# Moving all of GpSimd's work but a triangular inversion to ScalarE and VectorE in a hybrid decoder step

## The chip, the cores and the metric

One NeuronCore of one Trainium2 chip runs the whole program. The metric is device time in microseconds (us) from the first to the last instruction of one execution, with the small fixed part around it that the timer also sees. Lower is better. The times before come from three executions; the trace comes from one further execution with the hardware profiler on.

## The reference

One layer of a decoder runs over 1024 prompt tokens and 8 single-token samples, all in float32. RMSNorm of x, one input projection (1024 to 7688 columns), and then three branches whose outputs are gated, merged and projected back. The branch that this change touches is the gated delta branch:

```python
qkv, new_buf = causal_conv(conv_buf, concat([q, k, v]), conv_w)   # 4 taps, then SiLU
q = l2norm(q) * DK ** -0.5 ; k = l2norm(k)
L    = where(strict, (k * beta) @ k.T * decay, 0)                 # per chunk
Tinv = triangular_solve(eye + L, eye)                             # inverse of a lower triangle
u = Tinv @ (v * beta) ; w = Tinv @ (k * beta * exp(gc))
for each chunk:                                                   # state S: 128x128 per head
    v_new = u - w @ S
    o = q_dec @ S + attn @ v_new
    S = S * g_last + k_dec.T @ v_new
```

There are 4 heads of 128 by 128. For the 8 samples the same rule runs for one token on a given state (`state_delta`), and the new state is an output.

## The kernel before, in words

**Projections.** All heavy matmuls are float32 split in two rounded halves (hi and lo), so each output tile of 128 columns takes three passes over 8 contraction blocks (`mm3`, L299 to L304), for three groups of 344 tokens: 24 matmuls a group, 72 a job. A job's weights come by an ACT-queue DMA (`w_load`, L265), are cast to hi on ScalarE (L277) and subtracted to lo on VectorE (L280). Each group's PSUM bank (`pj`, two of them) is emptied by ScalarE or VectorE before a third group can use it.

**Order of the work.** The schedule is written out by hand: every engine executes its instructions in the order in which this Python emits them. After every 6 matmuls `mm3` calls `tick()` (L135), which advances each generator in `run.items` by one step, in the order in which they were added. `yield n` skips n further ticks. So the delta branch is strewn among the projection matmuls, and a TensorE instruction of the delta branch whose operand isn't ready holds all projection matmuls behind it. `run.until(cond)` ticks without projection matmuls until `cond` holds. The jobs run in the order of `plan_a`: k, v, q, then jobs of other branches, per head.

**The start (L526 to L628).** The first tiles k, v and bv of head 0 are projected from un-normed x while the norms are found; then q 0 and bv 1, while the normed x is split again into hTh (ScalarE) and hTl (VectorE, L188) by `n_again` (L445), one part of the tokens after another. After that `wab2` is split (L626) and the beta and alpha logits are projected (L658 to L666); `gates_gen` (L668) makes the gates from them.

**Convolution.** `qkv_tile` (L502) takes a raw tile `xraw` (128 x 1035, two buffers), clears its first three columns (L512, GpSimd) and returns the function that copies each projected group into it (L516 ScalarE, or L518 VectorE in the first head). With the last group `conv_gen` (L472) starts: for k and v four VectorE instructions over 1024 tokens (L489, L494), for q 14 GpSimd instructions over 512 tokens (L485, L487) with a scratch tile `cvt`; the 8 sample columns go through VectorE for all three (L490, L496). Then a wait in ticks (10 for q, 2 for k and v, L498), SiLU on ScalarE (L499), and the key is put in `done`.

**Per head.** `inverse_gen` (L842) waits for k, loads the cumulated log gates E, makes L on TensorE, ScalarE and VectorE (L860 to L880), writes its diagonal blocks to DRAM (`ld`, L885), waits in program order until `("dbc", h-1)` is done, and loads them back as `Lt` (L891). GpSimd clears X (L893 to L895) and runs the inversion of 32 x 32 blocks: 62 small instructions (L901, L907). Then `sample_gen` (L739) is added, X goes to DRAM (`ud`, L914) and comes back into U (L918); VectorE transposes blocks of it (L921 to L923) and TensorE completes the inverse (L929 to L954). `chunks_gen` (L962), added before the inversion, loads `gcb` (L969), transposes k (L978), takes the Exp of gcb on ScalarE (L982), waits in program order until q and v are done, copies the sample columns of k, q and v (`kqs`, `vss`, L990, L992, GpSimd), and makes A (L998), `ssq` (L1010) and r. `chain_gen` (L1034) then walks the 8 chunks.

**Samples.** `sample_gen` waits in program order for `kq_s[h]`, loads the head's state `st` (L745, one buffer, on the SP queue), multiplies kqs (L747 to L749), sums on TensorE (L752), normalizes on VectorE into `kqp` (L762), multiplies with the state on TensorE (L771), and ends with the state update (L814, L817), its store (L822) and `("dbc", h)`.

**DMA queues.** SP issues nearly all DMAs, in program order, and waits there for each one's operands: the order per head is E, ld (4), Lt (4), gcb, ud (4), U (4), st, the small sample transfers, the store of st, with output tiles of other jobs between. ACT issues the weight loads.

Of the kernel before, what the change touches and what calls it, by code (L numbers as in the profile page):

```python
# [12 lines left out]
F32 = mybir.dt.float32  # L13
# [3 lines left out]
ALU = mybir.AluOpType  # L17
# [4 lines left out]
P = 128  # L22
D = 1024
T = 1024
NB = 8
NT = T + NB
# [125 lines left out]
def tile_mixer_step(ctx: ExitStack, tc: tile.TileContext, a):  # L152
    nc = tc.nc
    V, S, G, PE, SP = nc.vector, nc.scalar, nc.gpsimd, nc.tensor, nc.sync
# [3 lines left out]
    done = set()  # L158
# [55 lines left out]
    ones = const.tile([P, P], F32, name="ones")  # L214
# [184 lines left out]
    xp = scoped(xst, "xp")  # L399
# [70 lines left out]
    xraw = {}  # L470

    def conv_gen(ti, dstk, raw, key):  # L472
        SP.dma_start(out=a["conv_new"][ti * P:(ti + 1) * P], in_=raw[:, T:T + 3 + NB])
        cw = [colv[:, c_cw + j * 12 + ti:c_cw + j * 12 + ti + 1] for j in range(4)]
        d = dstk[:, :T]
        s = scT[:, ti].rearrange("p (b j) -> p j b", j=3)
        e = dstk[:, T:NT]
        if key[0] == "q":
            tmp = xp.tile([P, T], F32, tag="cvt", name="cvt", bufs=1)
            for j in range(4):  # L480
                for c in range(0, T, 512):
                    cs = slice(c, c + 512)
                    x = raw[:, j + c:j + c + 512]
                    o = tmp[:, cs] if j else d[:, cs]
                    G.tensor_tensor(out=o, in0=x, in1=cw[j].to_broadcast([P, 512]), op=ALU.mult)  # L485
                    if j:
                        G.tensor_tensor(out=d[:, cs], in0=d[:, cs], in1=o, op=ALU.add)  # L487
        else:
            V.tensor_scalar(out=d, in0=raw[:, 0:T], scalar1=cw[0], scalar2=None, op0=ALU.mult)  # L489
        V.tensor_scalar(out=e, in0=s[:, 0], scalar1=cw[0], scalar2=None, op0=ALU.mult)  # L490
        yield
        for j in range(1, 4):
            if key[0] != "q":
                V.scalar_tensor_tensor(out=d, in0=raw[:, j:j + T], scalar=cw[j], in1=d, op0=ALU.mult, op1=ALU.add)  # L494
            x = s[:, j] if j < 3 else raw[:, 3 + T:3 + NT]
            V.scalar_tensor_tensor(out=e, in0=x, scalar=cw[j], in1=e, op0=ALU.mult, op1=ALU.add)  # L496
            yield 1
        yield 10 if key[0] == "q" else 2  # L498
        S.activation(out=dstk, in_=dstk, func=AF.Silu)  # L499
        done.add(key)  # L500

    def qkv_tile(name, h):  # L502
        if name == "k":
            kq_t[h] = xp.tile([P, 2, NT], F32, tag="kq", name="kq")
            v_t[h] = xp.tile([P, NT], F32, tag="vt", name="vt")
        ti, dstk = {
            "k": (4 + h, kq_t[h][:, 0]),
            "v": (8 + h, v_t[h]),
            "q": (h, kq_t[h][:, 1]),
        }[name]  # L510
        raw = xp.tile([P, 3 + NT], F32, tag="xraw", name="xraw", bufs=2)
        G.memset(raw[:, 0:3], 0.0)  # L512

        def evac(n, sl, o, scaled=True):
            if scaled:
                S.copy(out=raw[:, 3 + sl.start:3 + sl.stop], in_=o)  # L516
            else:
                V.tensor_tensor(out=raw[:, 3 + sl.start:3 + sl.stop], in0=o, in1=rbc[:, sl], op=ALU.mult)  # L518
            if n == NS - 1:
                run.add(conv_gen(ti, dstk, raw, (name, h)))  # L520

        return evac
# [96 lines left out]
    for n in range(4):  # L619
# [10 lines left out]
    dp = scoped(dst, "dp")  # L630
# [3 lines left out]
        out=mask, in_=mask, pattern=[[1, P]], compare_op=ALU.is_ge, fill=NEG, base=0, channel_multiplier=-1  # L634
# [3 lines left out]
        out=ut, in_=ones, pattern=[[1, P]], compare_op=ALU.is_ge, fill=0.0, base=0, channel_multiplier=-1  # L638
# [8 lines left out]
    ab = dp.tile([16, 9 * P], F32, tag="r", name="ab")  # L647
# [10 lines left out]
    for n in range(NS):  # L658
        sl = slice(n * NW, (n + 1) * NW)
        o = pj()[:16, :NW]  # L660
        for k in range(KT):
            PE.matmul(o, lhsT=wab2[:, k], rhs=hTh[:, k, sl], start=(k == 0), stop=False)
            PE.matmul(o, lhsT=wab2[:, k], rhs=hTl[:, k, sl], start=False, stop=(k == KT - 1))
            if k % 3 == 2:
                tick()
        S.copy(out=ab[:, sl], in_=o)  # L666

    def gates_gen():  # L668
        sel = dp.tile([16, 8], F32, name="sel")
# [69 lines left out]
    def sample_gen(h):  # L739
        while h not in kq_s:  # L740
            yield
        kq, vs = kq_s[h]
        ks, qs = kq[:, 0], kq[:, 1]
        st = dp.tile([P, NB, P], F32, tag="st", name="st")
        SP.dma_start(out=st, in_=a["state_delta"][:, h].rearrange("b k v -> k b v"))  # L745
        pr = sm.tile([P, 3, NB], F32, tag="pr", name="pr")
        V.tensor_tensor(out=pr[:, 0], in0=ks, in1=ks, op=ALU.mult)  # L747
        V.tensor_tensor(out=pr[:, 1], in0=qs, in1=qs, op=ALU.mult)
# [88 lines left out]
    hd = {}  # L837
# [4 lines left out]
    def inverse_gen(h):  # L842
# [46 lines left out]
        ldv = ld.rearrange("c b j i -> (c b) j i")  # L889
        for q in range(4):  # L890
            SP.dma_start(out=Lt[bsl[q]], in_=ldv)  # L891
        X = dp.tile([P, 8, 32], F32, tag="X", name="X")
        G.memset(X, 0.0)  # L893
        for q in range(4):
# [67 lines left out]
    def chunks_gen(h):  # L962

        while h and ("rec", h - 1) not in done:
            yield
        kq, vt = kq_t[h], v_t[h]
        E, ssk, cj, ck = (hd[h][n] for n in ("E", "ssk", "cj", "ck"))
        gcb = dp.tile([P, CC, P], F32, tag="gcb", name="gcb")
        SP.dma_start(out=gcb, in_=gcd[h * CC:(h + 1) * CC].rearrange("c i -> (c i)").partition_broadcast(P))  # L969
        Kg = dp.tile([P, CC, P], F32, tag="Kg", name="Kg")  # L970
        kd = dp.tile([P, CC, P], F32, tag="kd", name="kd")
        A = dp.tile([P, CC, P], F32, tag="A", name="A")
        hd[h].update(gcb=gcb, Kg=Kg, kd=kd, A=A)
        for cs in halves:
            t = bank()
            for c in range(4):
                cc = cs.start + c
                transpose(t[:, c], kq[:, 0, cc * P:(cc + 1) * P])  # L978
            V.tensor_tensor(out=Kg[:, cs], in0=t, in1=bc4(eg[:, h, cs]), op=ALU.mult)
            V.tensor_tensor(out=kd[:, cs], in0=t, in1=bc4(ck[:, cs]), op=ALU.mult)  # L980
            yield 1
        S.activation(out=gcb, in_=gcb, func=AF.Exp)  # L982
        nk = sm.tile([P, CC], F32, tag="nk", name="nk")
        yield from rsqrt_slow(nk, ssk, "nk")
        V.tensor_tensor(out=nk, in0=nk, in1=ssk, op=ALU.mult)
        while not {("q", h), ("v", h)} <= done:
            yield
        yield 1
        kqs = sm.tile([P, 2, NB], F32, tag="kqs", name="kqs")
        G.tensor_copy(out=kqs, in_=kq[:, :, T:NT])  # L990
        vss = sm.tile([P, NB], F32, tag="vss", name="vss")
        G.tensor_copy(out=vss, in_=vt[:, T:NT])  # L992
        kq_s[h] = (kqs, vss)
        for cs in halves:
            t = bank()
            for c in range(4):
                sl = slice((cs.start + c) * P, (cs.start + c + 1) * P)
                PE.matmul(t[:, c], lhsT=kq[:, 0, sl], rhs=kq[:, 1, sl], start=True, stop=True)  # L998
            for c in range(4):
                cc = cs.start + c  # L1000
                V.scalar_tensor_tensor(
                    out=A[:, cc], in0=t[:, c], scalar=cj[:, cc:cc + 1], in1=E[:, cc], op0=ALU.mult, op1=ALU.mult
                )
            yield 1
        qg = kq[:, 1, :T].rearrange("p (c i) -> p c i", c=CC)
        ssq = sm.tile([P, CC], F32, tag="ssq", name="ssq")
        for cs in halves:
            t = bank()
            for c in range(4):
                transpose(t[:, c], qg[:, cs.start + c])  # L1010
            for c in range(4):
                cc = cs.start + c
                S.activation(out=junk(), in_=t[:, c], func=AF.Square, accum_out=ssq[:, cc:cc + 1])
            yield 1
        V.tensor_tensor(out=gcb, in0=qg, in1=gcb, op=ALU.mult)
        yield
        V.tensor_scalar(out=ssq, in0=ssq, scalar1=EPS, scalar2=None, op0=ALU.add)
        rq = sm.tile([P, CC], F32, tag="rq", name="rq")
        yield from rsqrt_slow(rq, ssq, "rq")
        V.tensor_scalar(out=rq, in0=rq, scalar1=DKS, scalar2=None, op0=ALU.mult)  # L1020
        while h and ("turned", h - 1) not in done:
            yield
        r = dp.tile([P, CC, P], F32, tag="r", name="r")
        hd[h].update(r=r, rq=rq)
        for cs in halves:
            t = bank()
            for c in range(4):
                cc = cs.start + c
                transpose(t[:, c], vt[:, cc * P:(cc + 1) * P])
            V.tensor_tensor(out=r[:, cs], in0=t, in1=bc4(nk[:, cs]), op=ALU.mult)  # L1030
            yield
        done.add(("chunks", h))
# [518 lines left out]
    op = None  # L1551
# [112 lines left out]
```

## Time and profile before

| | |
|---|---|
| three executions, median (lowest to highest) | 1249.45 us (1248.71 to 1252.63) |
| the profiled execution | 1252.32 us |
| its span, first to last instruction | 1250.6 us |
| mean granted TensorE clock | 0.951 |
| TensorE matmuls busy | 1141.1 us (91%) |
| VectorE / ScalarE / GpSimd busy | 644.5 / 411.8 / 209.9 us |

How to read it: PE is TensorE, DVE is VectorE, ACT is ScalarE, POOL is GpSimd, SP issues DMAs; a q behind a name (SPq, ACTq) is that engine's sequencer. "L771" is line 771 of the kernel. The view of waits says how long an engine stood idle, in how many places, before instructions of a line, and what released it (an engine and line, or a DMA). A timeline row gives the start, the duration, the engine, the line, the operation, the tiles written and read, the shape and the count, and in brackets the idle time before it with its releaser. The view of windows gives, for a stretch of time, the busy time of each engine with its number of instructions and, as PEclk, the granted TensorE clock as a share of full speed. A view by form groups instructions: busy us, mean ns of one, and idle time before them. The chain of waits is followed back from the last instruction.

### The profile page before, as it was taken

How to read it: one execution, taken by the hardware profiler on the slowest of the kernel's cores; microseconds unless marked ns; L12 is line 12 of the kernel's file. 1: busy time of each engine (PE TensorE's matmuls, PEld its weight loads, DVE VectorE, ACT ScalarE, POOL GpSimd, SP SyncE). 2: the span in 40 equal slices, each digit the busy share in tenths (PEclk: the TensorE clock that was granted, in tenths of full speed). 3: DMA queues.
4: the chain of work that ended last, by engine and by line, in shares of the span. 5: the costliest groups of instructions: out<-in, count | busy, mean ns of one | idle time of the engine just before them, and what ended most of it. 6: DMA issues, size and time to landing. Idle time of an engine off the chain costs nothing.

```text
span 1250.6 us, 19297 instructions
## 1 busy us (share of the span) xinstructions
PE 1141.1 (91%) x7618; PEld 1091.1 (87%) x7618; DVE 644.5 (52%) x1637; ACT 411.8 (33%) x824; POOL 209.9 (17%) x392
## 2 busy tenths in 40 slices
PE   8969879879965898959999999989999999999997
PEld 8959878868965798959999999988999999999884
DVE  5992627454470636324315754264555335776554
ACT  7334313231341222323334432354444521222332
POOL 0071320650018100830001420010111000000000
PEclk8979988888988899879999999999999999999999
DMA  9103322222121222112254445544353255663321
GB/s 367 51 18 57 119 56 73 73 63 90 56 81 34 77 68 90 53 43 102 105 164 140 145 161 172 170 134 134 102 155 101 77 176 174 194 228 132 101 85 52
DMA packets 83612, 139.87 MB, mean 112 GB/s; under 512 B 21809, under 2 KB 51729, under 8 KB 82873
## 3 DMA queue, kind: packets, MB, share of 16 engines
q1 hardware_dynamic: 70112, 98.24, 24.3%
q10 hardware_dynamic: 13408, 40.39, 10.5%
q8 instruction: 60, 0.98, 0.3%
q14 instruction: 32, 0.25, 0.1%
HBM read 107.07 MB, written 31.64 MB: 111 GB/s over the span
## 4 chain that ended last, share of the span: by engine, by line
PE 69%; POOL 10%; DVE 9%; DMA 6%; issue 3%; SPq 2%; ACT 2%; POOLq 0%; DVEq 0%; ACTq 0%
PE pj L302 38%; PE dl L302 20%; POOL itmp L901 3%; POOL X L907 3%; POOL kq L487 2%; POOL cvt L485 2%; PE tp L225 1%; DVE xT L330 1%; DMA st<-state_delta 1%; DVE hTl L188 1%; PE dl L1282 1%; DMA ud<-X 1%; DVE vt L494 1%; DVE wlo L280 1%; SPq L918 1%
## 5 line engine op out<-in xcount | busy, mean ns | idle before, releaser
L302 PE MATMUL pj<-hTh,whi 128*128 128x344 f32 (+1 forms) x1384 | 275.8, 336 | 25.6 <-ACT xraw L516 15.1
L302 PE MATMUL pj<-hTh,wlo 128*128 128x344 f32 (+1 forms) x1384 | 265.0, 327 | 3.2 <-DVE wlo L280 3.2
L302 PE MATMUL pj<-hTl,whi 128*128 128x344 f32 (+1 forms) x1384 | 263.7, 328 | 0.0
L302 PEld LDWEIGHTS pj<-hTh,whi 128*128 128x128 f32 x1384 | 229.3, 197 | 30.0 <-ACT xraw L516 15.6
L302 PEld LDWEIGHTS pj<-hTh,wlo 128*128 128x128 f32 x1384 | 226.1, 192 | 4.7 <-DVE wlo L280 3.4
L302 PEld LDWEIGHTS pj<-hTl,whi 128*128 128x128 f32 x1384 | 229.1, 194 | 0.8 <-issue 0.2
L280 DVE TENSOR_TENSOR wlo<-raw,whi 128x1024 fp32r<-128x1024 f32 (+1 forms) x92 | 101.4, 1103 | 115.7 <-ACT whi L277 115.6
L277 ACT CAST whi<-raw 128x1024 fp32r<-128x1024 f32 (+1 forms) x92 | 86.1, 936 | 97.8 <-PE dl L302 69.1
L1106 ACT COPY stg<-pj 128x344 f32<-128x344 f32 x72 | 32.1, 446 | 125.2 <-PE pj L302 125.2
L302 PE MATMUL dl<-yh,wlo 128*128 128x344 f32 x288 | 57.4, 321 | 0.0
L302 PE MATMUL dl<-yl,whi 128*128 128x344 f32 x288 | 57.0, 320 | 0.0
L302 PE MATMUL dl<-yh,whi 128*128 128x344 f32 x288 | 57.0, 320 | 0.0
L1339 POOL TENSOR_TENSOR kvt<-kvt,qb 128x1024 f32<-128x1024 f32 x8 | 19.4, 2452 | 214.0 <-DMA kvt<-cache_mem_v 214.0
L901 POOL TENSOR_TENSOR itmp<-X,Lt 128x60 f32<-128x60 f32 (+24 forms) x124 | 39.4, 318 | 81.5 <-DMA Lt<-ld 72.3
L302 PEld LDWEIGHTS dl<-yh,whi 128*128 128x128 f32 x288 | 47.8, 188 | 0.0
L302 PEld LDWEIGHTS dl<-yl,whi 128*128 128x128 f32 x288 | 47.5, 188 | 0.0
L302 PEld LDWEIGHTS dl<-yh,wlo 128*128 128x128 f32 x288 | 47.5, 188 | 0.0
L907 POOL TENSOR_TENSOR X<-X,itmp 128x60 f32<-128x60 f32 (+24 forms) x124 | 38.9, 314 | 9.7
L1053 DVE COPY y<-dl 128x128 f32<-128x128 f32 x32 | 9.3, 289 | 55.9 <-PE dl L1051 46.7
L487 POOL TENSOR_TENSOR kq<-kq,cvt 128x512 f32<-128x512 f32 x24 | 35.9, 1498 | 1.9
L1066 ACT COPY r<-dl 128x128 f32<-128x128 f32 x32 | 8.5, 266 | 83.4 <-PE dl L1065 80.8
L512 POOL MEMSET xraw<- 128x3 f32 x12 | 1.0, 104 | 206.0 <-DVE kq L496 206.0
(396 smaller groups left out, 1730.8 us busy)
## 6 DMA issues: line engine op xcount, KB each, us to landing
raw<-w_tiles ACTq DMA_DIRECT2D x61, 512.0 KB, 3.8
gate<-stg SPq DMA_DIRECT2D x23, 516.0 KB, 3.2
stg<-gate SPq DMA_DIRECT2D x23, 516.0 KB, 3.6
raw<-w_br ACTq DMA_DIRECT2D x24, 256.0 KB, 3.7
x<-x_prompt SPq DMA_DIRECT2D x8, 512.0 KB
kvt<-cache_mem_k SPq DMA_DIRECT2D x16, 256.0 KB, 4.2
kvt<-cache_mem_v SPq DMA_DIRECT2D x16, 256.0 KB, 4.8
wor<-w_out SPq DMA_DIRECT2D x8, 512.0 KB
```

What stands on the lines that cost most here:

```text
L188: V.tensor_tensor(out=lo, in0=src, in1=f32(hi), op=ALU.subtract)
L225: PE.transpose(out, in_, ident[:p, :p])
L277: S.copy(out=hi, in_=raws[i])
L280: eng.tensor_tensor(out=lo, in0=raws[i], in1=f32(hi), op=ALU.subtract)
L302: PE.matmul(out, lhsT=w, rhs=r, start=(i == 0), stop=(i == len(ops) - 1))
L330: V.scalar_tensor_tensor(out=x[:, k], in0=x[:, k], scalar=colv[:, col + k:col + k + 1], in1=r, op0=ALU.mult, op1=ALU.mult)
L485: G.tensor_tensor(out=o, in0=x, in1=cw[j].to_broadcast([P, 512]), op=ALU.mult)
L487: G.tensor_tensor(out=d[:, cs], in0=d[:, cs], in1=o, op=ALU.add)
L901: G.tensor_tensor(out=tm, in0=X[:, 0:m, j:j + 1].to_broadcast([P, m, n]), in1=Lt[:, j:j + 1, j + 1:32].to_broadcast([P, m, n]), op=ALU.mult,)
L907: G.tensor_tensor(out=X[:, 0:m, j + 1:32], in0=X[:, 0:m, j + 1:32], in1=tm, op=ALU.subtract)
L1106: project("gate", i, lambda n, sl, o: S.copy(out=t[:, sl], in_=o))
L1339: G.tensor_tensor(out=kts[hb], in0=kts[hb], in1=qb[:, hb * 4:hb * 4 + 4].unsqueeze(2).to_broadcast([P, 4, 2, P]), op=ALU.mult,)
```

## The change

GpSimd keeps the clearing of X and the inversion in this part of the program. Six edits:

1. The q convolution is done as that of k and v, with four VectorE instructions over 1024 tokens; the scratch `cvt` goes. For q of head 0 it is held back in program order until the beta and alpha logits are copied out (`"ab"`).
2. The wait before SiLU is 2 ticks for q too, instead of 10.
3. The raw tile has three buffers instead of two.
4. The three zero columns are written by ScalarE, as a multiplication of ones by zero.
5. `kqs` and `vss` are copied by ScalarE.
6. The head's state `st` is loaded in `inverse_gen`, right behind the four Lt loads on the SP queue, instead of in `sample_gen`.

```diff
-        if key[0] == "q":
-            tmp = xp.tile([P, T], F32, tag="cvt", name="cvt", bufs=1)
-            for j in range(4):
-                for c in range(0, T, 512):
...
-                    G.tensor_tensor(out=o, in0=x, in1=cw[j].to_broadcast([P, 512]), op=ALU.mult)
-                    if j:
-                        G.tensor_tensor(out=d[:, cs], in0=d[:, cs], in1=o, op=ALU.add)
-        else:
-            V.tensor_scalar(out=d, in0=raw[:, 0:T], scalar1=cw[0], scalar2=None, op0=ALU.mult)
+        while key == ("q", 0) and "ab" not in done:
+            yield
+        V.tensor_scalar(out=d, in0=raw[:, 0:T], scalar1=cw[0], scalar2=None, op0=ALU.mult)
         V.tensor_scalar(out=e, in0=s[:, 0], scalar1=cw[0], scalar2=None, op0=ALU.mult)
         yield
         for j in range(1, 4):
-            if key[0] != "q":
-                V.scalar_tensor_tensor(out=d, in0=raw[:, j:j + T], scalar=cw[j], in1=d, op0=ALU.mult, op1=ALU.add)
+            V.scalar_tensor_tensor(out=d, in0=raw[:, j:j + T], scalar=cw[j], in1=d, op0=ALU.mult, op1=ALU.add)
...
-        yield 10 if key[0] == "q" else 2
+        yield 2
         S.activation(out=dstk, in_=dstk, func=AF.Silu)
...
-        raw = xp.tile([P, 3 + NT], F32, tag="xraw", name="xraw", bufs=2)
-        G.memset(raw[:, 0:3], 0.0)
+        raw = xp.tile([P, 3 + NT], F32, tag="xraw", name="xraw", bufs=3)
+        S.mul(out=raw[:, 0:3], in_=ones[:, 0:3], mul=0.0)
...
         S.copy(out=ab[:, sl], in_=o)
+    done.add("ab")
...
-        st = dp.tile([P, NB, P], F32, tag="st", name="st")
-        SP.dma_start(out=st, in_=a["state_delta"][:, h].rearrange("b k v -> k b v"))
+        st = hd[h]["st"]
...
             SP.dma_start(out=Lt[bsl[q]], in_=ldv)
+        st = hd[h]["st"] = dp.tile([P, NB, P], F32, tag="st", name="st")
+        SP.dma_start(out=st, in_=a["state_delta"][:, h].rearrange("b k v -> k b v"))
...
-        G.tensor_copy(out=kqs, in_=kq[:, :, T:NT])
+        S.copy(out=kqs, in_=kq[:, :, T:NT])
...
-        G.tensor_copy(out=vss, in_=vt[:, T:NT])
+        S.copy(out=vss, in_=vt[:, T:NT])
```

More of the change, by code (lines that the diff above doesn't have):

```diff
@@ L477, in conv_gen @@
         e = dstk[:, T:NT]
-        if key[0] == "q":
-            tmp = xp.tile([P, T], F32, tag="cvt", name="cvt", bufs=1)
-            for j in range(4):
-                for c in range(0, T, 512):
-                    cs = slice(c, c + 512)
-                    x = raw[:, j + c:j + c + 512]
-                    o = tmp[:, cs] if j else d[:, cs]
-                    G.tensor_tensor(out=o, in0=x, in1=cw[j].to_broadcast([P, 512]), op=ALU.mult)
-                    if j:
-                        G.tensor_tensor(out=d[:, cs], in0=d[:, cs], in1=o, op=ALU.add)
-        else:
-            V.tensor_scalar(out=d, in0=raw[:, 0:T], scalar1=cw[0], scalar2=None, op0=ALU.mult)
+        while key == ("q", 0) and "ab" not in done:
+            yield
+        V.tensor_scalar(out=d, in0=raw[:, 0:T], scalar1=cw[0], scalar2=None, op0=ALU.mult)
         V.tensor_scalar(out=e, in0=s[:, 0], scalar1=cw[0], scalar2=None, op0=ALU.mult)
```

## The prediction

> **What bounds the kernel now.** I read the page first: who is busy, and in which slices.
>
> ```profile
> span 1250.6 us, 19297 instructions
> PE 1141.1 (91%) x7618; PEld 1091.1 (87%) x7618; DVE 644.5 (52%) x1637; ACT 411.8 (33%) x824; POOL 209.9 (17%) x392
> PE   8969879879965898959999999989999999999997
> ```
>
> TensorE is busy for 1141 us of 1250.6, and its idle time lies in the first half, where the delta branch is strewn among the projections. So only idle time of TensorE can be won, some 109 us, and the time that it runs slowly behind it. The view of waits, for TensorE, says where:
>
> ```profile
> PE tp L752 <- DVE pr L749: 23.5, 2, 17.0
> PE pj L302 <- ACT xraw L516: 15.1, 2, 9.4
> PE tp L771 <- DMA st<-state_delta: 14.7, 3, 8.6
> PE pj L662 <- DVE wab L188: 8.3, 1, 8.3
> PE dl L929 <- DVE TA L921: 7.9, 1, 7.9
> ...
> PE dl L998 <- ACT kq L499: 3.9, 1, 3.9
> PE dl L1056 <- DVE y L1053: 3.7, 2, 3.5
> ```
>
> Total, times, longest. A wait costs more than its length: TensorE starts again at a low clock. The view of windows for the stretches right behind six stalls that I expect to go or shrink below 2 us (the first and the last of the six, and their sum):
>
> ```profile
> 90.00:95.00 5.00, 5.00 (x20) 2.53 (x21) 4.37 (x4) 0.28 (x1) 4.85 (x6) 0.55 0.29 107
> ...
> 550.00:555.50 5.50, 4.65 (x47) 4.51 (x48) 3.94 (x17) 0.82 (x2) 0.00 (x0) 0.52 0.68 201
> sum 28.00, PE 27.08 PEld 24.00 DVE 14.68 ACT 3.20 POOL 8.71; mean PE 4.51 PEld 4.00 DVE 2.45 ACT 0.53 POOL 1.45
> ```
>
> PEclk is 0.55 and 0.52 there: 27.08 us of matmuls at about 0.53 of the clock, which at full clock would take 0.47 x 27.08 = 12.7 us less.
>
> **GpSimd's queue (q convolution, kqs).** L752 waits for pr, pr for kqs, and kqs is copied by GpSimd in program order, behind the inversion; and the inversions of heads 1 and 2 stand behind the q convolution, though their operand is there long before. First SP's timeline, then GpSimd's (the first instruction of the inversion of each of these heads):
>
> ```profile
> 226.42 1.71 SPq L891 DMA_DIRECT2D Lt<-ld  x4
> ...
> 361.60 1.71 SPq L891 DMA_DIRECT2D Lt<-ld  x4
> ```
>
> ```profile
> 247.12 0.24 POOL L901 TENSOR_TENSOR itmp<-X,Lt 128x31 f32<-128x31 f32 x1
> ```
>
> ```profile
> 387.65 0.24 POOL L901 TENSOR_TENSOR itmp<-X,Lt 128x31 f32<-128x31 f32 x1
> ```
>
> The loads are issued 20.7 and 26.0 us before the first use. With some 4 us for issue and transfer (a state load of the same size takes 4.03, below), the inversions start 17 and 22 us sooner. TensorE comes sooner too, but only by what is saved in that head: L752's 6.5 or 17.0 us and its part of L771 and of the clock. So U keeps about the lead that it had. In head 3 the convolution stands in the middle of the inversion; that is the 7.9 us at L929 and, through SiLU of q, the 3.9 us at L998. On ScalarE kqs follows SiLU of its own q and v. All of L752 (23.5), L929 (7.9) and L998 (3.9) goes: **35.3 us**. What is late next is the inversion itself, with a spare time of several us, and behind it gcb (below).
>
> **The state.** st was queued on SP behind ud and U. Early, it has the whole inversion to land. Heads 1 and 2: 14.7 - 8.6 = **6.1 us** goes. In head 0 another wait stands right behind it (timelines of ScalarE, VectorE and TensorE):
>
> ```profile
> 169.94 1.04 ACT L277 CAST whi<-raw 128x1024 fp32r<-128x1024 f32 x1 [8.53 <-DMA ud<-X]
> ```
>
> ```profile
> 171.02 1.23 DVE L280 TENSOR_TENSOR wlo<-raw,whi 128x1024 fp32r<-128x1024 f32 x1 [6.80 <-ACT whi L277]
> ...
> 174.45 0.18 DVE L762 TENSOR_TENSOR kqp<-kqs,rn 128x16 f32<-128x16 f32 x1
> ```
>
> ```profile
> 177.39 1.03 PE L771 MATMUL tp<-st,kqp 128*32 128x128 f32 x13 [8.61 <-DMA st<-state_delta]
> ```
>
> ScalarE's weight load and cast were held until ud had landed, VectorE stood behind the cast, and kqp, L771's other operand, came at 174.6. So L771 can start at 174.7, and **2.7 us** of 8.6 goes, with no clock won.
>
> **The start.** While GpSimd convolves q of head 0, VectorE's instructions with two SBUF operands take nearly twice as long:
>
> ```profile
> 69.01 1.21 DVE L280 TENSOR_TENSOR wlo<-raw,whi 128x1024 fp32r<-128x1024 f32 x1
> ...
> 70.73 1.96 DVE L496 SCALAR_TENSOR_TENSOR kq<-scT,colv,kq 128x8 f32<-128x8 f32 x2
> ...
> 72.95 4.13 DVE L188 TENSOR_TENSOR hTl<-xT,hTh 128x1024 fp32r<-128x1024 f32 x2
> ...
> 86.66 2.06 DVE L280 TENSOR_TENSOR wlo<-raw,whi 128x1024 fp32r<-128x1024 f32 x1
> 88.64 1.28 DVE L188 TENSOR_TENSOR wab<-wab,wab 128x64 fp32r<-128x64 f32 x1
> ```
>
> wlo takes 1.21 us alone and 2.06 beside GpSimd, the pair of hTl 4.13 where 2 x 1.21 = 2.42 is due. Three such pairs lie ahead of wab: 3 x 1.7 = 5.1; wlo 0.85; wab about 1.0 (64 columns); and the q sample columns, 1.96, move behind the logits: 8.9 us, more than the stall. But the third pair needs ScalarE's casts, which hang on TensorE's pace:
>
> ```profile
> 78.28 2.00 ACT L187 CAST hTh<-xT 128x1024 fp32r<-128x1024 f32 x2 [0.86 <-PE pj L302]
> ```
>
> They end at 80.3; then half a pair 1.2, wlo 1.2 and wab 0.25: 82.95 instead of 89.9, **7.0 us** less, and a stall of about 1.3 stays.
>
> **What it adds.** On VectorE per head one L489 and three L494 (view by form, kq, 100 to 620 us):
>
> ```profile
> L494 DVE SCALAR_TENSOR_TENSOR kq<-xraw,colv,kq 128x1024 f32<-128x1024 f32 x9 | 11.5, 1279 | 0.0
> ...
> L489 DVE TENSOR_SCALAR kq<-xraw,colv 128x1024 f32<-128x1024 f32 x3 | 2.3, 750 | 1.1 <-ACT xraw L516 1.1
> ```
>
> 4 x (0.75 + 3 x 1.28) = 18.4 us on an engine that is 52% busy. Behind them in its queue stand wlo and, in head 1, the copies y of the chain. k's same instructions already stand in chains, and the row of L1056 above shows one wait of 3.5 and one of 0.2 for y. So I bound the meeting of q and chain between 0 and 3 x 1.28 = 3.8 us and take 1.0. q of head 0 puts two of its steps among the gates' small instructions: 0 to 2.6 us, taken as 0.2, since the other two fall into VectorE's idle time ahead of them. On ScalarE there are 20 small instructions more; the nearest row is its smallest copy:
>
> ```profile
> L1066 ACT COPY r<-dl 128x128 f32<-128x128 f32 x32 | 8.5, 266 | 83.4 <-PE dl L1065 80.8
> ```
>
> 20 x 0.27 = 5.3 us over 500 us, hidden: ScalarE is 33% busy. The clearing waits for a raw tile's last reader, three tiles ago, and only copies into that tile stand behind it: nothing.
>
> **The third raw tile** looks like the cure for the 15.1 us at L516, but isn't by these rows. On SP and ScalarE, head 2:
>
> ```profile
> 363.82 0.43 SPq L969 DMA_DIRECT2D gcb<-gcd  x1
> ```
>
> ```profile
> 369.06 1.06 ACT L982 ACTIVATE gcb<-gcb 128x1024 f32<-128x1024 f32 x1 [6.32 <-DMA gcb<-gcd]
> ```
>
> The copy into xraw stood on ScalarE behind an Exp that waited for gcb. The 15.1 us stay. They grow, for the state now goes ahead of gcb on SP: between 0.43 us (one more issue) and the whole time of a state load, from the chain:
>
> ```profile
> 416.14 4.03 DMA st<-state_delta
> ```
>
> Both move 512 KB and can overlap; I take the middle, 2.2 us, in heads 2 and 3: 4.4 us lost. In head 1 gcb is loaded much later; in head 0 TensorE waits for the inversion afterwards anyway. New on SP: st waits until the store of the head before has read its one buffer, with gcb and output tiles behind it. That store is issued ahead of Lt, so this costs nothing.
>
> **The inversion beside VectorE.** One GpSimd row with and one without VectorE's convolution of v beside it:
>
> ```profile
> 504.02 0.29 POOL L901 TENSOR_TENSOR itmp<-X,Lt 128x50 f32<-128x50 f32 x1
> 504.38 1.13 POOL L907 TENSOR_TENSOR X<-X,itmp 128x50 f32<-128x50 f32 x1
> ```
>
> Each L494 beside the inversion costs it about 0.85 us; three heads x 3 = 7.6 us if all of it reached TensorE. I take 0, as the inversion starts 17 us or more sooner in heads 1 and 2 and is no longer broken in two in head 3.
> The Trainium skill (SBUF — State Buffer, Who interferes with whom) speaks against the change here: a VectorE instruction with two SBUF inputs and a GpSimd instruction that reads SBUF exclude each other for a whole instruction. By that rule a step could cost its full 1.28 us, 11.5 us over three heads, and the time would be 1203 if that reached TensorE; the rows agree in kind, with 0.85.
>
> **The sum.** Won: 35.3 + 6.1 + 2.7 + 7.0 + 12.7 (clock) = 63.8. Lost: 4.4 + 1.0 + 0.2 = 5.6. Net 58.2 us. The profiled execution took 1252.32 (1.7 outside its span) and gives 1194.1; it lay 2.9 above the median of 1249.45, from which I count: **1191 us**. Bounds of this case: if L771 of head 0 gains nothing (+2.7), gcb costs 4.0 twice (+3.6) and half of the 7.6 and the 3.8 is seen (+6), 1203; if gcb costs 0.4 (-3.6) and the stall at wab goes wholly (-1.3), 1186.
>
> **Rivals.**
> 1. ScalarE takes the place of GpSimd. SiLU of q comes 8 ticks sooner, and if VectorE is behind with the convolution, ScalarE stands, and with it the copies out of PSUM and the kqs. For it: ScalarE already waits 6.3 us for a DMA in this way. Against: VectorE stood idle while GpSimd convolved q of head 2. Three heads at about 3 us beyond what two banks cover, and 2.5 us of clock each: +16.5, **1208**. Chance 0.17.
> 2. More goes than I count: the 15.1 us at L516 go too, because VectorE, no longer held by GpSimd, gives L and so ld, Lt and gcb sooner. Against it: gcb still stands behind Lt and st. 1191.3 - 15.1 - 4.4 = **1172**. Chance 0.11.
> 3. Slower: the inversion's operand, not GpSimd's queue, sets L752, L929 and L998. Then none of the 35.3 and 8.8 goes; the start still wins 7.0 + 2.4 of clock. gcb costs 4.0 in three heads (12.1), VectorE's steps the full 7.6 and 3.8: 23.5 - 9.4 = +14, **1263**. It decides if Lt lands no sooner than the first instruction of the inversion; the rows above have it issued 21 and 26 us before. Chance 0.05.
> 4. It does not do what it says: the early st and kqs only let TensorE run into the next wait of the same head, and gains and losses cancel, within 0.3% of the median (about what a measurement can tell from no change, 3.7 us): **1249**. Chance 0.04.
>
> **The numbers.** My case has the remaining 0.63. Faster by over 0.3%: 0.63 + 0.17 + 0.11 = 0.91; the same 0.04; slower 0.05. The range reaches from between my case and rival 2 to the upper end of rival 1: 1174 to 1212.
>
> **What would show it.** In the changed profile, GpSimd's first L901 of heads 1 to 3 should follow Lt by some 4 us, and waits at L752, L998 and L929 be gone, each under 2 us. hTl pairs should take 2.4 us and L662 wait under 2. L771 should wait for kqp in head 0, some 5 us, and nowhere for st. L516 should still show two waits, together 15 to 23 us, behind the Exp at L982. I am wrong if TensorE waits at L929 in more than one head, if VectorE's y or kqp delay it in many places, or if L516's waits vanish.

## The result, and the profile after

| | before | after |
|---|---|---|
| median (lowest to highest), four runs each | 1250.66 us (1248.71 to 1252.63) | 1194.38 us (1192.78 to 1197.37) |
| ratio of the two, 95% interval | | 0.955 (0.9525 to 0.958) |
| the profiled execution | 1252.32 us | 1195.52 us |
| mean granted TensorE clock | 0.951 | 0.972 |

The change wins 56.3 us. In the kernel after, the lines behind the edited convolution are numbered 8 to 10 lower: L771 of before is L761, L752 is L742, L929 is L921, L998 is L990, L516 is L506, the Exp L982 is L974, the inversion L901 and L907 is L893 and L899, the load of the state is L883, that of gcb L961, the store of X to `ud` L906.

The page of the kernel after, the three lines that answer to those shown of before:

```profile
span 1193.8 us, 19219 instructions
PE 1129.0 (95%) x7618; PEld 1080.2 (90%) x7618; DVE 645.1 (54%) x1653; ACT 414.0 (35%) x844; POOL 145.8 (12%) x316
PE   8989798999969997999999999899999999999997
```

TensorE's idle time fell from 1250.6 - 1141.1 = 109.5 us to 1193.8 - 1129.0 = 64.8, and the same 7618 matmuls took 12.1 us less. GpSimd gave up 64 us. VectorE's busy time is what it was (644.5 before), although it took over the convolution of q, which the prediction puts at 18.4 us; some 5 us of what it no longer loses are seen at the start (three pairs of hTl, below).

The view of waits for TensorE (total, times, longest):

```profile
PE pj L302 <- ACT xraw L506: 19.2, 2, 11.4
PE pj L302 <- ACT stg L1120: 8.2, 2, 6.8
PE dl L1048 <- DVE y L1045: 3.7, 2, 3.6
...
PE pj L302 <- ACT agt L1116: 2.7, 1, 2.7
...
PE tp L742 <- DVE pr L739: 1.6, 1, 1.6
...
PE tp L761 <- DVE kqp L752: 1.6, 1, 1.6
...
PE pj L652 <- DVE wab L188: 1.4, 1, 1.4
...
PE tp L702 <- DVE gp L698: 1.2, 1, 1.2
```

Of the five waits that were to go, L742's is 1.6 where it was 23.5, those of L921 and L990 are off the list, L761 waits once for kqp and never for st, and wab is 1.4 where it was 8.3. The two largest that are left are ScalarE's: both are copies out of PSUM that stand behind the Exp of gcb, as the experiments show.

The inversion now starts as soon as its operand is there. SP's timeline and GpSimd's, heads 1 and 2:

```profile
210.06 1.71 SPq L881 DMA_DIRECT2D Lt<-ld  x4
...
328.44 1.71 SPq L881 DMA_DIRECT2D Lt<-ld  x4
```

```profile
214.06 0.24 POOL L893 TENSOR_TENSOR itmp<-X,Lt 128x31 f32<-128x31 f32 x1 [48.94 <-DMA Lt<-ld]
...
332.76 0.24 POOL L893 TENSOR_TENSOR itmp<-X,Lt 128x31 f32<-128x31 f32 x1 [85.18 <-DMA Lt<-ld]
```

4.0 and 4.3 us from issue to first use, where it was 20.7 and 26.0; the releaser is now the load itself (head 3 has 4.3 too, 450.71 to 455.00). At the start, VectorE's timeline shows the pairs of hTl at 2.35 us, where they took 4.13 beside GpSimd:

```profile
71.07 2.35 DVE L188 TENSOR_TENSOR hTl<-xT,hTh 128x1024 fp32r<-128x1024 f32 x2
...
81.24 0.22 DVE L188 TENSOR_TENSOR wab<-wab,wab 128x64 fp32r<-128x64 f32 x1
```

### The profile page after: what moved, and what is told of

Its sections match the earlier page's. It is cut to its first block, busy times and chain, and to the rows that moved or that the text cites. A ratio compares the mean times of both kernels' runs of the same rounds, so it can differ in the third digit from the quotient of the medians.

```text
span 1193.8 us, 19219 instructions
## 1 busy us (share of the span) xinstructions
PE 1129.0 (95%) x7618; PEld 1080.2 (90%) x7618; DVE 645.1 (54%) x1653; ACT 414.0 (35%) x844; POOL 145.8 (12%) x316
## 4 chain that ended last, share of the span: by engine, by line
PE 73%; DVE 11%; POOL 6%; DMA 5%; issue 2%; ACT 2%; SPq 1%; ACTq 0%; POOLq 0%; DVEq 0%
PE pj L302 41%; PE dl L302 21%; POOL X L899 3%; POOL itmp L893 3%; PE tp L225 1%; DVE xT L330 1%; DVE wlo L280 1%; DVE kq L484 1%; PE dl L1274 1%; DMA Lt<-ld 1%; PE dl L1048 1%; DVE L L868 1%; DVE vt L484 1%; PE tp L1226 1%; DMA ld<-L 1%
## 5 line engine op out<-in xcount | busy, mean ns | idle before, releaser
L302 PE MATMUL pj<-hTh,whi 128*128 128x344 f32 (+1 forms) x1384 | 273.4, 333 | 35.7 <-ACT xraw L506 19.2
L302 PEld LDWEIGHTS pj<-hTh,whi 128*128 128x128 f32 x1384 | 225.7, 194 | 40.9 <-ACT xraw L506 19.7
L893 POOL TENSOR_TENSOR itmp<-X,Lt 128x60 f32<-128x60 f32 (+24 forms) x124 | 46.5, 375 | 287.4 <-DMA Lt<-ld 278.0
L1331 POOL TENSOR_TENSOR kvt<-kvt,qb 128x1024 f32<-128x1024 f32 x8 | 19.4, 2450 | 213.9 <-PE pj L302 93.3
L899 POOL TENSOR_TENSOR X<-X,itmp 128x60 f32<-128x60 f32 (+24 forms) x124 | 43.9, 354 | 9.7
L1514 DVE TENSOR_TENSOR stg<-dl,stg 128x344 f32<-128x344 f32 x48 | 24.7, 514 | 18.0 <-PE dl L302 18.0
L302 PE MATMUL dl<-woh,mh 128*128 128x512 f32 x128 | 31.8, 390 | 0.0
```

What stands on the lines that cost most here:

```text
L302: PE.matmul(out, lhsT=w, rhs=r, start=(i == 0), stop=(i == len(ops) - 1))
L893: G.tensor_tensor(out=tm, in0=X[:, 0:m, j:j + 1].to_broadcast([P, m, n]), in1=Lt[:, j:j + 1, j + 1:32].to_broadcast([P, m, n]), op=ALU.mult,)
L899: G.tensor_tensor(out=X[:, 0:m, j + 1:32], in0=X[:, 0:m, j + 1:32], in1=tm, op=ALU.subtract)
L1331: G.tensor_tensor(out=kts[hb], in0=kts[hb], in1=qb[:, hb * 4:hb * 4 + 4].unsqueeze(2).to_broadcast([P, 4, 2, P]), op=ALU.mult,)
L1514: V.tensor_tensor(out=sg[:, sl], in0=o, in1=sg[:, sl], op=ALU.mult)
```

## The experiments

The theory: GpSimd executes in program order; the q convolution ahead of the inversion and the inversion ahead of kqs made TensorE wait, and only the edits together remove that. The rivals: the new work on ScalarE or VectorE costs as much as a part of the change wins; the third raw tile or the early state has a large share; VectorE's convolution beside the inversion reaches TensorE after all.

**The change again**, as the yardstick of its batch.

> The changed kernel once more, as the measure for the runs beside it. 1194 us, within 3.

Measured: 1192.68 us (1187.47 to 1195.26), ratio 0.9523 (0.9497 to 0.9548). Two batches of the same kernel differ by 0.3%.

**One part alone: the copies on ScalarE.** The kernel before, with

```diff
-        G.tensor_copy(out=kqs, in_=kq[:, :, T:NT])
+        S.copy(out=kqs, in_=kq[:, :, T:NT])
...
-        G.tensor_copy(out=vss, in_=vt[:, T:NT])
+        S.copy(out=vss, in_=vt[:, T:NT])
```

> The kernel before with one part of the change: kqs and vss copied by ScalarE. The 23.5 us at L752 go. My theory: nearly nothing is won by it alone, since L771 behind it waits for the state, which lands at 283.1 and 420.2 us whatever TensorE does, just when L771 ran before: 0 to 3 us, 1248 to 1251. Rival (the waits add up as the view of waits lists them): 23.5 us and 4 of clock won, 1223.

Measured: 1253.0 us, ratio 1.001 (0.9994 to 1.0025): nothing. Its waits for TensorE:

```profile
PE tp L771 <- DMA st<-state_delta: 40.9, 3, 22.7
PE pj L302 <- ACT xraw L516: 15.0, 2, 9.7
```

The 23.5 us at L752 are gone, and the wait for st is 26.2 us longer. The state is queued on SP behind the stores of X, hence behind the inversion, so TensorE meets the late inversion one instruction group later. This is what the prediction's fourth rival describes, for this part of the change alone. A wait that vanishes from the list is not yet time won.

**One part alone: the start.** The kernel before, with q of head 0 convolved on VectorE behind the logits:

```diff
-        if key[0] == "q":
+        while key == ("q", 0) and "ab" not in done:
+            yield
+        pool_conv = key[0] == "q" and key[1] > 0
+        if pool_conv:
```

> The kernel before with one part of the change: the convolution of q of head 0 alone goes to VectorE, behind the logits. My theory (in the start VectorE's two-operand instructions are held by GpSimd's convolution): L662 starts 8.4 us sooner, as in the changed kernel, 2 us more come from the clock behind it, and the gates lose 1: 9 to 11 us won, 1240 to 1242 of 1250.7. Rival (the start is bound by ScalarE's casts or TensorE's pace, not by GpSimd): under 3 us.

Measured: 1241.15 us against 1250.76, ratio 0.9919 (0.99 to 0.9938): 9.6 us won. In its list of waits wab has 1.4 us where it had 8.3, and st 12.6 where it had 14.7, together 9.0. The 2 us of clock that I expected on top did not come: TensorE's busy time is 1141.0 us, against 1141.1. This part stands by itself.

**All but the convolution.** The kernel before, with the clearing and the copies on ScalarE and the state loaded behind Lt; the q convolution stays on GpSimd, with two raw tiles:

```diff
-        G.memset(raw[:, 0:3], 0.0)
+        S.mul(out=raw[:, 0:3], in_=ones[:, 0:3], mul=0.0)
...
-        st = dp.tile([P, NB, P], F32, tag="st", name="st")
-        SP.dma_start(out=st, in_=a["state_delta"][:, h].rearrange("b k v -> k b v"))
+        st = hd[h]["st"]
...
+        st = hd[h]["st"] = dp.tile([P, NB, P], F32, tag="st", name="st")
+        SP.dma_start(out=st, in_=a["state_delta"][:, h].rearrange("b k v -> k b v"))
...
-        G.tensor_copy(out=kqs, in_=kq[:, :, T:NT])
+        S.copy(out=kqs, in_=kq[:, :, T:NT])
...
-        G.tensor_copy(out=vss, in_=vt[:, T:NT])
+        S.copy(out=vss, in_=vt[:, T:NT])
```

> The kernel before with only the clearing and the copies on ScalarE and the early state; the q convolutions stay on GpSimd, with two raw tiles. My theory (the queue of GpSimd is what counts): the start loses its gain (about 10 us), the inversions of heads 1 and 2 start 17 and 22 us later again, so that TensorE, not held at L752 any more, waits for U instead in head 2, and L998 and L929 of head 3 keep their 12 us with their clock: 1222 to 1240. Rival (kqs and the state are the whole gain behind the start): 1204, the changed kernel plus the start alone.

Measured: 1235.18 us against 1251.99, ratio 0.9861 (0.9834 to 0.9888). Its waits:

```profile
PE dl L931 <- DVE TA L923: 19.4, 2, 9.8
PE pj L302 <- ACT xraw L516: 18.1, 2, 11.0
PE tp L771 <- DVE kqp L762: 9.8, 2, 7.1
PE pj L662 <- DVE wab L188: 8.4, 1, 8.4
```

16.8 of the 56 us. The waits for pr and st are gone, and TensorE stands 19.4 us at the first use of the inverse (L931) instead: the inversion still starts late. So some 39 us hang on the convolution leaving GpSimd, with the shorter wait ahead of SiLU, which was not tried alone; the start alone was worth 9.6. The clearing, the copies and the early state win 16.8 us without it.

**The third raw tile.** The kernel after, with two:

```diff
-        raw = xp.tile([P, 3 + NT], F32, tag="xraw", name="xraw", bufs=3)
+        raw = xp.tile([P, 3 + NT], F32, tag="xraw", name="xraw", bufs=2)
```

> The changed kernel with two raw tiles instead of three. My theory (the copies into xraw wait behind the Exp for gcb, not for a raw tile): no change, 1194 within 2. Rival (the third tile is part of the gain): waits at xraw beyond 19.2 us and at least 4 us more, 1198 or above.

Measured: 1194.82 us, ratio 0.9546 (0.9524 to 0.9569), whose interval overlaps that of the change again, and 17.9 us of waits for xraw where that has 18.0. The third tile buys nothing that can be measured.

**The state, late again.** The kernel after, with the state loaded in `sample_gen`, as before:

```diff
-        st = hd[h]["st"]
+        st = dp.tile([P, NB, P], F32, tag="st", name="st")
+        SP.dma_start(out=st, in_=a["state_delta"][:, h].rearrange("b k v -> k b v"))
```

> The changed kernel with the state load put back to its old place, behind ud and U on SP. My theory (the early state is worth little once the inversions end early, and it costs time ahead of gcb): in the changed kernel the last U load is issued at 166, 249, 367 and 493 us, and a state load takes 4.0, so it would land at 170, 253, 371 and 497 where L771 (now L761) ran at 165, 254, 374 and 496: about +5 in head 0, nothing in heads 1 and 2, +1 in head 3. The two waits behind gcb shrink by 2.0 and 2.1. Together +2 us, 1194 to 1199. Rival (the state edit is worth what the wait of 14.7 us in the profile before says): +9 to +15, 1203 to 1209.

Measured: 1201.45 us, ratio 0.9598 (0.9572 to 0.9624), 8.8 us more than the change again. Its waits:

```profile
PE pj L302 <- ACT xraw L506: 15.2, 2, 9.3
PE tp L762 <- DMA st<-state_delta: 15.0, 3, 7.0
PE tp L743 <- DVE pr L740: 4.2, 1, 4.2
```

The waits behind gcb fall back to 15.2 us, the size they had before the change: the early state does cost them some 3 to 4 us. But the wait for st is back in full at 15.0 us, as long as in the kernel before. The 2 us that I expected were too few: as I read it now, a TensorE that is held for less time at gcb comes to L762 sooner, and I had left that out.

**The state right behind gcb.** The kernel after, with the state's load moved from behind Lt to behind gcb's:

```diff
         SP.dma_start(out=gcb, in_=gcd[h * CC:(h + 1) * CC].rearrange("c i -> (c i)").partition_broadcast(P))
+        st = hd[h]["st"] = dp.tile([P, NB, P], F32, tag="st", name="st")
+        SP.dma_start(out=st, in_=a["state_delta"][:, h].rearrange("b k v -> k b v"))
```

> The changed kernel with the state load issued right behind gcb instead of ahead of it. My theory: the waits at xraw in heads 2 and 3 fall from 11.4 and 7.8 back to about 9.4 and 5.7, 4.1 us in all; in head 0 the wait of 6.8 before L771 falls to about 3.2, but kqp is no sooner, so a wait of the same size comes back at L771 and nothing is won there. About 1190, 1188 to 1192. Rival (the state's place does not touch gcb; the waits grew for another reason): no change, 1194.

Measured: 1189.08 us, ratio 0.9502 (0.9479 to 0.9525). The 3.6 us less than the change again are near the size expected, but the intervals overlap, and the mechanism that I gave is refuted: its profile shows 18.1 us for xraw where the change again has 18.0. The timelines of SP and ScalarE say why. In heads 2 and 3, us from the issue of the Lt loads to the start of the Exp of gcb, which in every one of these rows was released by gcb's landing:

| kernel | place of the state's load | head 2 | head 3 | waits for xraw |
|---|---|---|---|---|
| before | behind U | 7.5 | 5.6 | 15.1 |
| state late | behind U | 8.1 | 5.6 | 15.2 |
| change, again | ahead of gcb | 8.9 | 7.3 | 18.0 |
| change | ahead of gcb | 10.1 | 7.2 | 19.2 |
| state right behind gcb | behind gcb | 8.7 | 7.7 | 18.1 |

Ahead of gcb or right behind it, the state costs gcb about as much. So, as far as these rows show, it is not the place in SP's order that delays gcb, but that both loads, of 512 KB each, are under way at the same time. Where the 3.6 us come from is left open.

**The Exp of gcb, later.** The kernel after, with one line moved:

```diff
-        S.activation(out=gcb, in_=gcb, func=AF.Exp)
         nk = sm.tile([P, CC], F32, tag="nk", name="nk")
...
+        S.activation(out=gcb, in_=gcb, func=AF.Exp)
         qg = kq[:, 1, :T].rearrange("p (c i) -> p c i", c=CC)
```

> The changed kernel with the Exp of gcb emitted later, just ahead of the squares, so that ScalarE does not stand for gcb's DMA while copies into xraw wait behind it. My theory: the 19.2 us at xraw vanish, and with them some 4 us of low clock; but TensorE then reaches the results of the inversions of heads 2 and 3 sooner, and waits for kqp or U come back for about half: 8 us won in head 2 and 4 in head 3, 1182 (1176 to 1187). Rival (the copies wait for the raw tile or VectorE, not for this Exp): no change, 1194.

Measured: 1167.45 us (1165.55 to 1172.76), ratio 0.9331 (0.9301 to 0.9361): far beyond what I expected, and faster than both kernels. Its page and the first of its waits, with one further down (the profiled execution took 1172.76 us, the longest of the four):

```profile
PE 1126.4 (96%) x7618; PEld 1077.9 (92%) x7618; DVE 648.6 (55%) x1653; ACT 415.2 (35%) x845; POOL 145.3 (12%) x316
```

```profile
PE dl L921 <- DVE TA L913: 6.4, 2, 3.2
PE pj L302 <- DVE ql L188: 4.6, 1, 4.6
PE dl L1048 <- DVE y L1045: 3.7, 2, 3.5
...
PE pj L302 <- ACT stg L1120: 0.5, 1, 0.5
```

The waits for xraw (19.2) are gone, and of the 8.2 us for stg at L1120 0.5 are left: the 6.8 us of head 0 stood behind the same Exp. Those of agt, pr and kqp, 5.9 us together, are off the list too. What comes is 6.4 us at L921: now the inversion is last. I had counted on a larger part of the waits moving there.

**Both moves, and the later Exp with two raw tiles.** The diffs are those above, combined.

> Both: the Exp of gcb emitted later, and the state load issued behind gcb. My theory: as the late Exp alone, since nothing waits for gcb any more: within 2 us of that run, about 1182. Rival (the two gains add): 1178 or below.

> The later Exp of gcb with two raw tiles instead of three. With the Exp out of the way of the copies into xraw, the third tile could now be worth something. Theory that it is never the raw tile's last reader that is late: the same time as with the later Exp alone, ratio 0.930 to 0.937 (exp late alone: 0.933), no wait for xraw. Rival: the third tile was what let the waits at xraw vanish: they come back, 5 us or more, ratio above 0.938.

Measured: with the state behind gcb 1169.48 us, ratio 0.934 (0.9306 to 0.9374); with two raw tiles 1169.73 us, ratio 0.9335 (0.9318 to 0.9353), and no wait for xraw. Neither can be told from the later Exp alone. The third tile does nothing that can be measured even where the Exp no longer hides it.

**VectorE beside the inversion.** Two raw tiles, and in the convolution of q of heads 1 to 3 nine spare VectorE instructions with two SBUF operands; then, in their place, 18 with one. The spare results are read by nothing.

```diff
+            if key[0] == "q" and key[1]:
+                V.tensor_tensor(out=spare, in0=raw[:, j:j + T], in1=d, op=ALU.add)
```

```diff
+            if key[0] == "q" and key[1]:
+                for _ in range(2):
+                    V.tensor_scalar(out=spare, in0=raw[:, j:j + T], scalar1=cw[j], scalar2=None, op0=ALU.mult)
```

> The changed kernel with two raw tiles and, in heads 1 to 3, each of the three two-operand steps of the q convolution followed by a further VectorE instruction of the same size with two SBUF operands into a spare tile, so nine instructions of about 1.2 us more. My theory (VectorE and the inversion have several us to spare): the inversions get up to 2.6 us longer, and the time rises by 0 to 2 us over that with two raw tiles. Rival (each such instruction holds GpSimd for its whole length and the inversion is last): up to 11 us more, 1203 or above.

> Two raw tiles and, in the q convolution of heads 1 to 3, 18 spare VectorE instructions with one SBUF operand each (18 x 0.75 = 13.5 us more of VectorE's time, against about 11 us for the nine spare instructions with two operands, which cost 8 us). Theory that those 8 us came from two-operand instructions holding GpSimd's inversion: the inversions keep the lengths that they have with two raw tiles alone (ends near 243, 362 and 486 us), the time stays within 3 us of that kernel's 0.955 of the kernel before. Rival, VectorE's own time (kqp, y, pr and the low halves of weights stand longer in its queue): 8 to 10 us more, 0.961 to 0.963, with waits of TensorE for VectorE's y, pr and kqp grown though the inversions are not.

Measured: 1202.72 us, ratio 0.9612 (0.9579 to 0.9645), and 1201.73 us, ratio 0.9595 (0.957 to 0.9621); with two raw tiles alone 0.9546. My expectation of 0 to 2 us for the first is wrong: it is some 8, near what the rival said. (The two profiled executions, of nine spare and of two raw tiles alone, differ by only 4.0 us, so the waits below cover half of it.) The second was meant as a control that leaves GpSimd alone, and isn't one. The busy lines of the three pages, two raw tiles, nine spare, 18 spare:

```profile
PE 1126.8 (94%) x7618; PEld 1078.1 (90%) x7618; DVE 645.1 (54%) x1653; ACT 414.0 (35%) x844; POOL 145.2 (12%) x316
```

```profile
PE 1127.8 (94%) x7618; PEld 1078.8 (90%) x7618; DVE 657.0 (55%) x1662; ACT 413.8 (35%) x844; POOL 153.5 (13%) x316
```

```profile
PE 1130.6 (94%) x7618; PEld 1081.2 (90%) x7618; DVE 659.1 (55%) x1671; ACT 413.9 (34%) x844; POOL 152.3 (13%) x316
```

GpSimd, with the same 316 instructions, is busy for 8.3 us more beside nine instructions with two operands (0.92 each) and for 7.1 us more beside 18 with one (0.39 each). The Trainium skill (SBUF — State Buffer, Who interferes with whom) says that a `tensor_scalar` can enter a two-port mode, in which it excludes GpSimd as well, and the 7.1 us agree. So both kernels hold the inversion about equally, and both add 12 to 14 us to VectorE's queue; what the time owes to the one and to the other isn't separated by them. The largest waits of nine spare but that for xraw:

```profile
PE pj L302 <- ACT agt L1120: 6.5, 1, 6.5
PE pj L302 <- ACT stg L1124: 6.4, 2, 5.4
PE dl L1052 <- DVE y L1049: 5.7, 4, 3.5
PE tp L746 <- DVE pr L743: 4.6, 1, 4.6
```

With two raw tiles alone, agt has 5.0, y 3.7 and pr 2.2 us. The growth of agt can't be read: it is 2.7 and 3.9 in two profiles of the change itself, and 4.1 beside 18 spare. pr grows by 2.4 us (4.4 beside 18 spare) and stands behind the end of the inversion (next section); y grows by 2.0 (6.1 beside 18) and stands in VectorE's own queue.

## Why the prediction was right, and where it failed

The forecast was 1191 us, and the profiled execution was to take 1194.1; it took 1195.52, and the median is 1194.38. For GpSimd's queue, the largest term, the mechanism is shown: the releaser of the inversion's first instruction is now Lt, the two experiments that leave the convolution of heads 1 to 3 on GpSimd have 1235 and 1241 us, and the waits named went. Term by term, in us of TensorE's time, from the two lists of waits:

| step | predicted | measured |
|---|---|---|
| L752, L929, L998 | 35.3 | 33.7 (1.6 left at L742) |
| L771, heads 1 and 2 | 6.1 | 6.1 |
| L771, head 0 | 2.7 | 3.4 (below) |
| the start | 7.0 | 6.9 |
| clock | 12.7 | 12.1 (busy time of PE) |
| gcb behind st | -4.4 | -4.1 (xraw, 15.1 to 19.2) |
| chain's y | -1.0 | 0.0 |
| gates | -0.2 | -1.2 (gp) |
| inversion beside VectorE | 0 | agt, new, -2.7 |

The measured column adds up to 54.2 us of the 56.8 by which the profiled spans differ; the rest lies in small waits. That the forecast of 58.2 is so near is in part luck: y and small waits made up for the gates and agt.

At the start the size is right, but not the bound that I took it from. wab was ready at 81.5, not 82.95, for ScalarE's casts came sooner as well; TensorE came 1.5 us sooner too, so its wait shrank by 6.9 and the start by 8.4.

For gcb I took the middle between one more issue and a whole state load, 2.2 us; 2.7 and 1.6 were measured in heads 2 and 3 (the table among the experiments). That sum was a choice that came out well. What sets the cost is that the two loads are under way together, and hardly the place ahead of gcb.

In head 0 the price of L771 came out near for a reason that I gave only half: TensorE waits 1.6 us for kqp, not "some 5", because it is first held for 6.8 us at stg, behind an Exp whose gcb now comes after st; before it had been 3.2 there. 8.6 - 1.6 - 3.6 = 3.4 us. "In head 0 TensorE waits for the inversion afterwards anyway" is true of this kernel, but no floor: with the later Exp both waits go.

**The step that failed** is "I take 0, as the inversion starts 17 us or more sooner". The price of one instruction was nearly right: 0.85 us predicted, 0.92 measured with the spare ones. But more than three stand beside an inversion. In head 2 it took 22.1 us before, from its first instruction (387.65) to the issue of the first store of X,

```profile
409.79 2.97 SPq L914 DMA_DIRECT2D ud<-X  x4
```

and takes 26.5 after (332.76 to 359.22, below): 4.3 us more, beside the four instructions of q's convolution and one wlo, where VectorE had only a few small ones before. That none of it would reach TensorE was wrong. GpSimd's timeline in head 3, and VectorE's beside it:

```profile
470.27 0.33 POOL L899 TENSOR_TENSOR X<-X,itmp 128x64 f32<-128x64 f32 x1
...
471.40 1.33 POOL L899 TENSOR_TENSOR X<-X,itmp 128x75 f32<-128x75 f32 x1
472.81 1.25 POOL L893 TENSOR_TENSOR itmp<-X,Lt 128x70 f32<-128x70 f32 x1
```

```profile
471.26 1.27 DVE L484 SCALAR_TENSOR_TENSOR kq<-xraw,colv,kq 128x1024 f32<-128x1024 f32 x1
...
473.81 1.33 DVE L484 SCALAR_TENSOR_TENSOR kq<-xraw,colv,kq 128x1024 f32<-128x1024 f32 x1
```

A step that takes 0.33 us in the first row takes 1.33 beside an instruction of 1.27 us. The Trainium skill (SBUF — State Buffer, Who interferes with whom) describes this as an exclusive lock: one engine holds it for a whole instruction, and the other fully blocks. These rows agree; that the mean is 0.92 is probably because some of VectorE's time falls into gaps between GpSimd's instructions. The way from there to TensorE is not the inverse itself, which had the spare time that I gave it, but ScalarE's queue. SP's stores of X and ScalarE's timeline:

```profile
359.22 2.52 SPq L906 DMA_DIRECT2D ud<-X  x4
...
485.42 2.52 SPq L906 DMA_DIRECT2D ud<-X  x4
```

```profile
361.23 0.34 ACTq L269 DMA_DIRECT2D raw<-w_tiles  x1
361.61 0.20 ACT L982 COPY kqs<-kq 128x16 f32<-128x16 f32 x1 [10.78 <-DMA ud<-X]
361.72 0.19 ACT L984 COPY vss<-vt 128x8 f32<-128x8 f32 x1
361.81 1.04 ACT L277 CAST whi<-raw 128x1024 fp32r<-128x1024 f32 x1
362.76 0.45 ACT L1116 ACTIVATE agt<-pj 128x344 f32<-128x344 f32 x1
...
487.42 0.33 ACTq L269 DMA_DIRECT2D raw<-w_tiles  x1
487.80 0.20 ACT L982 COPY kqs<-kq 128x16 f32<-128x16 f32 x1 [6.13 <-DMA ud<-X]
```

A weight load, which reads nothing of X, goes out 2.0 us after the first store of X was issued, and the profile names that store's landing as what ended ScalarE's idle time. Behind it in program order stand kqs, a cast, and the copy of agt that empties a PSUM bank. So the end of the inversion sets ScalarE's next copies, and through them the 2.7 us at agt (head 2) and the 1.6 at pr (head 3). With the 4.3 us less of before, agt's copy in head 2 would have ended at some 358.9, and TensorE came for its bank at 360.6: an estimate from the rows, not tried. The kernel before showed the same hold at 169.94, and I had quoted that row without asking where else it would bite.

Of the rivals, ScalarE in GpSimd's place did not come as described: TensorE has no wait at L990, where SiLU of q would show. What was argued in the second rival for VectorE's sake, that the waits at L516 go as well, did not come with the change; the later Exp shows that they were to be had, by an edit of ScalarE's order. The third rival's condition, an operand that lands no sooner than the inversion used to start, is refuted by the rows at 214.06 and 332.76. The gates' 1.2 us are, as I read them, VectorE's steps of q among their small instructions; that is within the bounds of 0 to 2.6, with too little taken.

## What to carry to other kernels

When an engine that executes in order does two jobs, look for the small instruction that stands behind a long one, and move the whole chain of late operands together: the copies alone won nothing, all but the convolution 16.8 us, the whole 56. Then ask which instruction of the relieved queues still waits for a late operand with copies out of PSUM behind it: moving one Exp won some 25 us more, while the third buffer beside it won nothing. A step that holds another engine's instructions costs what hangs on that engine's last result, DMA queues included, and not only what reads that result.

## What the runs showed of the hardware

Three things that I had not expected, or not at this size.

Two loads of 512 KB that are under way together each take longer. SP's and ScalarE's rows of gcb in head 3, first with the state's load ahead of it (kernel after), then with the state loaded later (kernel before):

```profile
452.46 0.42 SPq L883 DMA_DIRECT2D st<-state_delta  x1
452.93 0.57 SPq L961 DMA_DIRECT2D gcb<-gcd  x1
```

```profile
457.90 1.06 ACT L974 ACTIVATE gcb<-gcb 128x1024 f32<-128x1024 f32 x1 [14.37 <-DMA gcb<-gcd]
```

```profile
497.30 0.42 SPq L969 DMA_DIRECT2D gcb<-gcd  x1
```

```profile
501.12 1.06 ACT L982 ACTIVATE gcb<-gcb 128x1024 f32<-128x1024 f32 x1 [12.27 <-DMA gcb<-gcd]
```

From gcb's issue to its Exp it is 5.0 us beside the state and 3.8 without (3.9 in the kernel with the state late); in head 2 it is 6.1 to 7.3 beside it, in three kernels, and 5.2 and 5.9 without. The state itself lands 4.0 us after its issue in the kernel before, and 7.6 after it where it is issued right behind gcb. It is gcb's landing that the Exp, and ScalarE's queue with it, waits for.

A load on ScalarE's queue was issued only when an unrelated store on SP's had landed (361.23 and 487.42 above, 2.0 us after the stores at 359.22 and 485.42). That the two share what signals their completion would explain it; this was not tried.

Right behind a long stall the clock was granted at half. The view of windows for the 5 us behind the 11.35 us stall at gcb in head 2 (engines' busy time with their counts, then PEclk):

```profile
340.00:345.00 5.00, 5.00 (x17) 5.00 (x18) 4.93 (x9) 2.64 (x3) 4.53 (x7) 0.50 0.26 90
```

0.50 of the clock over 5.00 us of matmuls: by my estimate 2.5 us more on top of the wait. With the later Exp, TensorE's busy time in all fell by 2.6 us (1129.0 to 1126.4).
